# A decoder step on one core: the residual add before the FFN on VectorE alone, its squares summed behind the last block, the third norm's root spread one column block later

## The chip, the cores and the metric

The kernel runs on one core of a Trainium2 chip. The metric is the time of one execution on the device, in microseconds (us); the figure for the kernel before is the median of three executions. A profile of one execution, taken by the hardware profiler, lists every instruction with its start and its length. The engines are named as in the profile: PE is TensorE's matmul, PEld its weight load, DVE is VectorE, ACT is ScalarE, POOL is GpSimd, and SP issues most DMAs.

## What is computed

One inference step of one decoder layer, for 256 prompt tokens and 8 sequences of 8 new tokens: 320 tokens, width 2048, all in float32. Cut to the part around the change:

```python
def decoder_layer(x, ssm_state, ssm_conv_state, ffn_conv_state, p):
    h = rms_norm(x, p["norm_mix_pre"])
    ...                              # two head groups, from h
    mix = jnp.concatenate([gate_out, ssm_out], axis=-1) @ p["w_out"]
    x = x + rms_norm(mix, p["norm_mix_post"])          # called x1 below
    f, new_ffn_conv = conv_ffn(rms_norm(x, p["norm_ffn_pre"]), ffn_conv_state, ...)
    x = x + rms_norm(f, p["norm_ffn_post"])

def conv_ffn(h, conv_state, w_up, conv_w, conv_b, w_down):
    up = h @ w_up                                      # 2048 -> 2 x 5632 columns
    up, new_conv = causal_depthwise_conv(up, conv_state, conv_w, conv_b)
    g, u = jnp.split(up, 2, axis=-1)
    return (jax.nn.gelu(g, approximate=True) * u) @ w_down, new_conv
```

`rms_norm(x, w)` is `x * rsqrt(mean(x*x) + 1e-6) * w`. The norm that the FFN reads (the third of the layer's four) has its token factor, the rsqrt, pulled out: the kernel multiplies x1 by the weight alone, projects that, and multiplies the projected columns by the factor, called `r3`, when it reads them out of PSUM.

## The kernel before, and what sets the order

Everything is held transposed: 128 of the 2048 features lie on the partitions, the 320 tokens along the free axis, so x1 is 16 blocks of 128 x 320 (`acc[:, kt, :]`, kt from 0 to 15).

**Products.** float32 products are made of three passes: each weight tile and each activation block is split into a rounded part `hi` and the remainder `lo`, and `accumulate` (L126 to L130) adds hi·hi (L128), hi·lo (L129) and lo·hi (L130) in PSUM. `slab` (L110) fetches one weight tile of 128 x 1024, i.e. eight blocks of 128 x 128: a DMA issued by SP into `wraw` (L115), a cast on ACT to `whi` (L117), a subtraction on DVE to `wlo` (L119). Each has three buffers, so ACT may cast tile n + 3 only when PE is done with tile n. Eight blocks of three passes are 24 matmuls.

**The first six column blocks.** `project` (L152) is called at L1030 for the FFN's first group. It makes four column blocks of the gate half, and, with `more`, two of the other half, in 12 weight tiles: x1's blocks 0-1, 2-3, then the two extra columns for blocks 0-3, then 4-5, 6-7, the extra columns for 4-7, and 8-9, 10-11, extra for 8-11; the last four blocks, 12-15, come in two tiles for the four columns and one for the extra. The results stay in PSUM (`late=up0`, six banks: four of pool `mm`, two of pool `ms`, which has four as well).

**x1's blocks.** `x1_ready` (L1017) makes them a cut ahead: DVE scales the mix by weight and by the second norm's factor, which lies in PSUM (L1022); an add of x, loaded by SP into `xr` in four parts with two buffers (`load_x`, L1013, issue at L1015), gives x1 (L1023), on DVE for blocks 0 and 1 and on POOL for the other 14; `split` makes `h_hi` on ACT (L343) and `h_lo` on DVE (L344). A part of `xr` is reloaded when the last of its four adds is done.

**Squares.** For the third norm, ACT squares each x1 block and POOL adds the even ones up in `sq3`, DVE the odd ones in `sq3b` (`add_square`, L276 to L282, called at L1034). They are queued behind the add of block 11.

**Seventh and eighth column blocks, root and spread.** `ffn_up(0)` (L1086 to L1108) makes them one by one, two weight tiles each: `ps_one` in a bank of pool `ms`, `ps_other` in one of pool `mm`. Written behind half of the seventh block are two `token_sums` (L258, ones-products over the partitions, L263), one for `sq3` and one for `sq3b`; `rsqrt_by_root` (L237) with DVE's L243 and L244, a square root on ACT, a reciprocal and a Newton step on DVE; behind the seventh block, `spread` (L267) transposes the result on PE (L271) and ACT copies it to `r3` (L273). `evac` (L1054) then reads each column block out of PSUM times `r3` (L1062, L1063) and goes on to the convolution and the gelu. The eighth block's bank comes free with the first `evac`; the next group's `project` needs four banks of `mm`.

**Order.** Each engine works through its own queue in order. A planner fixes the queues ahead of time: of what is ready by its own estimate it takes the work with the highest priority, then the earliest in the code. `first()` is the highest, the weight tiles and x1's blocks share the next, everything else comes in the order of the code. `tc.issue_after(ins)` queues the instructions in its block behind `ins` on the same engine, without a wait.

Of the kernel before, what the change touches and what calls it, by code (L numbers as in the profile page):

```python
# [17 lines left out]
P = 128  # L18
# [3 lines left out]
NT = NP + NS  # L22
D = 2048
KD = D // P
# [10 lines left out]
def hybrid_step(  # L35
# [10 lines left out]
    act, dve, pool, pe, sp = nc.scalar, nc.vector, nc.gpsimd, nc.tensor, nc.sync  # L46
# [6 lines left out]
    tp = ctx.enter_context(tc.tile_pool(name="tp", bufs=2))  # L53
# [11 lines left out]
    with tc.high_priority(offset=300000):  # L65
        dve.memset(ones, 1.0)

        ps = misc("early")
# [31 lines left out]
    def col(i):  # L100
        return prm[:, i:i + 1]


    def first():

        return tc.high_priority(offset=200000)
# [19 lines left out]
    def accumulate(ps, w, xhi, xlo, first, last):  # L126
        whi, wlo = w
        pe.matmul(ps, whi, xhi, start=first, stop=False)  # L128
        pe.matmul(ps, whi, xlo, start=False, stop=False)  # L129
        return pe.matmul(ps, wlo, xhi, start=False, stop=last).ins  # L130
# [4 lines left out]
    hT = [None, None]  # L135
# [60 lines left out]
    acc = None  # L196
# [37 lines left out]

    rsqrt_ins, sums_ins = [], []

    def rsqrt_by_root(rest, ps, scale, rows=P):  # L237

        v = tp.tile([P, 3], F32, tag="rs_v3", name="rs_v")[:rows]
        r = tp.tile([P, 3], F32, tag="rs_r3", name="rs_r", bufs=3)[:rows]  # L240
        t = tp.tile([P, 3], F32, tag="rs_t3", name="rs_t")[:rows]
        s = tp.tile([P, 3], F32, tag="rs_s3", name="rs_s")[:rows]
        dve.tensor_scalar(out=v, in0=rest, scalar1=scale, scalar2=EPS, op0=ALU.mult, op1=ALU.add)  # L243
        dve.scalar_tensor_tensor(out=v, in0=ps, scalar=scale, in1=v, op0=ALU.mult, op1=ALU.add)  # L244
        act.activation(s, v, AF.Sqrt)
        dve.reciprocal(r, s)
        dve.scalar_tensor_tensor(out=t, in0=v, scalar=-0.5, in1=r, op0=ALU.mult, op1=ALU.mult)
        dve.tensor_tensor(out=t, in0=t, in1=r, op=ALU.mult)
        rsqrt_ins.append(dve.scalar_tensor_tensor(out=r, in0=t, scalar=1.5, in1=r, op0=ALU.add, op1=ALU.mult).ins)
        return r  # L250
# [7 lines left out]
    def token_sums(*sqs):  # L258

        ps = misc("tsum")  # L260
        for c, o in enumerate((0, P, NT - P)):
            for i, sq in enumerate(sqs):
                ins = pe.matmul(ps[:, c:c + 1], sq[:, o:o + P], ones[:, 0:1], start=i == 0, stop=i == len(sqs) - 1).ins  # L263
        sums_ins.append(ins)
        return ps[:, 0:3]

    def spread(r, out=None):  # L267

        ps = misc("spread")
        for c, o in ((2, NT - P), (0, 0), (1, P)):  # L270
            pe.transpose(ps[:, o:o + P], r[:, c:c + 1].to_broadcast([P, P]), ident)  # L271
        if out is not None:
            act.copy(out, ps[:, :NT])  # L273
        return ps[:, :NT]

    def add_square(total, x, begins, adder=pool, place=("sq", 2)):  # L276
        if begins:
            act.activation(total, x, AF.Square)
        else:
            sq = tp.tile([P, NT], F32, tag=place[0], name="sq", bufs=place[1])  # L280
            act.activation(sq, x, AF.Square)
            adder.tensor_tensor(out=total, in0=total, in1=sq, op=ALU.add)  # L282

    def squares_of(total):
# [3 lines left out]
        def step(nb):  # L288
# [3 lines left out]
            with first():  # L292
# [5 lines left out]
                if nb > KD - 3:  # L298
# [12 lines left out]
    acc = hp.tile([P, KD, NT], F32, name="acc_mix")  # L311
# [3 lines left out]
    prm_at = dict(zip(("norm", "sc", "fw0", "fw1", "fw2", "fb"),  # L315
                      ((0, KD, 2 * KD, 3 * KD), (4 * KD, 4 * KD + 96), *((4 * KD + 120 + 2 * NF * i,) for i in range(4)))))
# [20 lines left out]
    def split(hi, lo, x, scale=None):  # L337

        if scale is None:
            act.copy(hi, x)  # L340
            dve.tensor_tensor(out=lo, in0=x, in1=hi.bitcast(F32), op=ALU.subtract)
        else:
            act.activation(hi, x, AF.Copy, scale=scale)  # L343
            dve.scalar_tensor_tensor(out=lo, in0=x, scalar=scale, in1=hi.bitcast(F32), op0=ALU.mult, op1=ALU.subtract)  # L344

    def out_parts(pool_, name):
        return (pool_.tile([P, 4, NT], F32R, tag=f"{name}hi", name=f"{name}hi"),
# [14 lines left out]
    with ExitStack() as mctx:  # L362
        op = mctx.enter_context(tc.tile_pool(name="op", bufs=1))
# [138 lines left out]
        with tc.tile_pool(name="gp", bufs=1) as gp:  # L502
# [11 lines left out]
            k = 0  # L514
# [168 lines left out]
            hi, lo = res  # L683


        with tc.tile_pool(name="sd", bufs=1) as sd:
# [8 lines left out]
            for c in range(4):  # L695
                ps = misc("bt_ps")
# [14 lines left out]
            rest = []  # L711
# [256 lines left out]
            norm = heads_out(0, 2, 2)  # L968
# [3 lines left out]
            norm = heads_out(1, 2, 2)  # L972
# [3 lines left out]
            norm = heads_out(2, 2, 3)  # L976
# [16 lines left out]
            with first():  # L993
                with tc.issue_after(pd_last[-1]):
                    made = next(rest[0])
                with tc.issue_after(made):
                    most = token_sums(sq2)
                with tc.issue_after(sums_ins[-1]):
                    ps = token_sums(*one)
                with tc.issue_after(sums_ins[-1]):  # L1000
                    made = next(rest[1])
                r = rsqrt_by_root(most, ps, 1.0 / D)
                behind = rsqrt_ins[-1]
                with tc.issue_after(behind):
                    next(rest[1])
                with tc.issue_after(made):
                    r2b = spread(r)
            sq3 = hp.tile([P, NT], F32, tag="ssq", name="sq3")


            xr, added = {}, []

            def load_x(q):  # L1013
                xr[q] = op.tile([P, 4, NT], F32, tag="xs", name="xr", bufs=2)
# [2 lines left out]
            def x1_ready(k0, nk):  # L1017
                for kt in range(k0, k0 + nk):
                    q, k = kt // 4, kt % 4
                    a = acc[:, kt, :]  # L1020
                    with first() if kt < 2 else tc.high_priority(offset=100000):
                        dve.scalar_tensor_tensor(out=a, in0=a, scalar=col(prm_at["norm"][0] + kt), in1=r2b, op0=ALU.mult, op1=ALU.mult)  # L1022
                        added.append((dve if kt < 2 else pool).tensor_tensor(out=a, in0=a, in1=xr[q][:, k, :], op=ALU.add).ins)  # L1023
                        split(hT[0][:, kt, :], hT[1][:, kt, :], a, col(prm_at["norm"][1] + kt))
                        if k == 3 and q < 2:
                            load_x(q + 2)
            load_x(0)
            load_x(1)
            up0 = []
            project(ffn_w_up, 0, None, late=up0, ready=x1_ready, after=behind, ahead=1, more=DFF, held=added)  # L1030
            sq3b = tp.tile([P, NT], F32, tag="pv", name="sq3b", bufs=4)
            with tc.issue_after(added[11]):
                for kt in range(KD):
                    add_square((sq3, sq3b)[kt % 2], acc[:, kt, :], kt < 2, (pool, dve)[kt % 2], ("pv", 4))  # L1034
    x1 = acc


    with tc.tile_pool(name="fp", bufs=1) as fp:
        r3 = fp.tile([P, NT], F32, name="r3")
# [4 lines left out]
        def ffn_up(g):  # L1044
            fst = fp.tile([P, 2, 4, NB, 2], F32, tag="fst", name="fst", bufs=2)
            for half in range(2):
                k = NF * half + 4 * g
# [3 lines left out]
            hi = fp.tile([P, 4, NT], F32R, tag="fhi", name="fhi", bufs=2)  # L1051
# [34 lines left out]
            if g == 0:  # L1086

                ps = misc("ps_one")
                for i in range(2):
                    wb = slab(rows_of(ffn_w_up, 8 * i, 8, DFF + 256, P))  # L1090
                    for k in range(8):
                        kt = 8 * i + k
                        accumulate(ps[:, :NT], wb(k, 0), hT[0][:, kt, :], hT[1][:, kt, :], kt == 0, kt == KD - 1)
                    if i == 0:
                        with first():
                            r = rsqrt_by_root(token_sums(sq3), token_sums(sq3b), 1.0 / D)
                with first():
                    spread(r, r3)
                up0.append((None, 6, ps))
                for _, j, ps in up0:  # L1100
                    evac(j // 4, j % 4, ps)
                ps = mm.tile([P, 512], F32, tag="mm", name="ps_other")
                for i in range(2):
                    wb = slab(rows_of(ffn_w_up, 8 * i, 8, DFF + 384, P))
                    for k in range(8):
                        kt = 8 * i + k
                        accumulate(ps[:, :NT], wb(k, 0), hT[0][:, kt, :], hT[1][:, kt, :], kt == 0, kt == KD - 1)
                evac(1, 3, ps)  # L1108
            else:
                for half in range(2):  # L1110
                    project(ffn_w_up, DFF * half + 512 * g, lambda j, ps: evac(half, j, ps))

            for half in range(2):
                k = NF * half + 4 * g
# [14 lines left out]
        for g in range(NG):  # L1129
            hi, lo = nxt  # L1130
            if g < NG - 1:
                nxt = ffn_up(g + 1)
            if g == 0:
                acc = fp.tile([P, KD, NT], F32, name="acc_ffn")
# [15 lines left out]
        with tc.issue_after(pd_last[-1]):  # L1150
            most = token_sums(sq4)
        with tc.issue_after(sums_ins[-1]):
            made = hand_over(banks, 0)
        with tc.issue_after(made):
            ps = token_sums(*one)
        r = rsqrt_by_root(most, ps, 1.0 / D)
        with tc.issue_after(sums_ins[-1]):
            made = hand_over(banks, 1, 2)
        with tc.issue_after(made):
# [105 lines left out]
```

## Time and profile before

| | |
|---|---|
| executions, us | 1821.31, 1821.66, 1822.76 |
| median, us | 1821.66 |
| span of the profiled execution, first to last instruction, us | 1821.3 |
| mean granted TensorE clock | 0.993 |
| weight bytes and other reads from HBM, MB | 277.80 |

The profiled execution's span is given and not its full time; the three executions lie 0.0 to 1.5 us above that span. Rows of the profile are read like this: a group has its line, engine, operation, the tiles written and read with their shapes, the count, then busy us and mean ns of one, then the engine's idle time just ahead of them and what ended it. A row of a timeline has start, length, engine, line, operation; a bracket holds the idle time before it and who ended it. "PEclk" is the share of full TensorE clock that the throttle granted.

### The profile page before, as it was taken

Reading aid. Unit: us, or ns where it says so; the run is one execution under the profiler, and the core shown is the slowest. Engines: PE = TensorE matmul, PEld = TensorE weight load, DVE = VectorE, ACT = ScalarE, POOL = GpSimd, SP = SyncE. Lnnn points to the kernel's source line nnn. Section 1 sums busy time; section 2 is a strip of 40 time slices with the busy share of each in tenths; the row PEclk is TensorE's granted clock in tenths of the full one; section 3 lists DMA queues with packets and bytes.
Section 4 is the critical chain, followed back from the end, with each engine's and each line's share of the span. In section 5 each row is a group of like instructions: output and inputs, shape, how many; then the busy total and the mean of one; then the engine's idle time right before and its main releaser. Section 6 shows DMA issues by size and latency. Waiting matters only on the chain.

```text
span 1821.3 us, 31186 instructions
## 1 busy us (share of the span) xinstructions
PE 1789.4 (98%) x12222; PEld 1751.6 (96%) x12222; DVE 1182.3 (65%) x2029; ACT 798.1 (44%) x1102; POOL 304.5 (17%) x626
## 2 busy tenths in 40 slices
PE   8999999999999999999899999999999999999998
PEld 8999999999889899999899999999999999999997
DVE  5449664557977868677776465647465665756575
ACT  6444454334535445444455433333334343433334
POOL 3102200000331312104521010101111010101004
PEclk9999999999999999999999999999999999999999
DMA  8656544455566565556454545444545445454542
GB/s 268 186 150 189 159 132 152 155 157 176 189 192 189 162 196 173 156 159 206 148 149 151 150 153 153 151 152 151 153 152 154 150 154 150 151 148 153 151 154 99
DMA packets 222947, 294.66 MB, mean 162 GB/s; under 512 B 16752, under 2 KB 150736, under 8 KB 222608
## 3 DMA queue, kind: packets, MB, share of 16 engines
q1 hardware_dynamic: 210544, 270.21, 48.6%
q10 hardware_dynamic: 9872, 14.82, 2.2%
q0 software_dynamic: 2384, 7.64, 1.4%
q8 instruction: 96, 1.57, 0.4%
q14 instruction: 51, 0.42, 0.1%
HBM read 277.80 MB, written 14.82 MB: 161 GB/s over the span
## 4 chain that ended last, share of the span: by engine, by line
PE 88%; DVE 4%; DMA 2%; issue 2%; POOL 2%; ACT 1%; ACTq 0%; POOLq 0%; DVEq 0%
PE ps L128 18%; PE ps L130 18%; PE ps L129 18%; PE pd L128 9%; PE pd L130 9%; PE pd L129 9%; DVE wlo L119 1%; PE y_ps L888 1%; DMA cT<-in_x_tok 1%; POOL acc_mix L1023 1%; ACT whi L117 1%; DMA cs<-dacs_d 1%; DMA st<-in_state_ssm 0%; POOL st L808 0%; PE sg L650 0%
## 5 line engine op out<-in xcount | busy, mean ns | idle before, releaser
L119 DVE TENSOR_TENSOR wlo<-wraw,whi 128x1024 fp32r<-128x1024 f32 (+1 forms) x476 | 592.0, 1244 | 455.4 <-ACT whi L117 452.8
L117 ACT CAST whi<-wraw 128x1024 fp32r<-128x1024 f32 (+1 forms) x476 | 496.3, 1043 | 730.2 <-PE ps L129 443.7
L128 PE MATMUL ps<-h_hi,whi 128*128 128x320 f32 x2528 | 787.5, 312 | 8.6 <-ACT whi L117 5.6
L130 PE MATMUL ps<-h_hi,wlo 128*128 128x320 f32 x2528 | 783.9, 310 | 4.3 <-DVE wlo L119 4.3
L129 PE MATMUL ps<-h_lo,whi 128*128 128x320 f32 x2528 | 782.8, 310 | 0.0
L128 PEld LDWEIGHTS ps<-h_hi,whi 128*128 128x128 f32 x2528 | 477.5, 189 | 14.2 <-ACT whi L117 6.9
L130 PEld LDWEIGHTS ps<-h_hi,wlo 128*128 128x128 f32 x2528 | 477.2, 189 | 6.6 <-DVE wlo L119 6.4
L129 PEld LDWEIGHTS ps<-h_lo,whi 128*128 128x128 f32 x2528 | 477.5, 189 | 0.7 <-issue 0.5
L128 PE MATMUL pd<-fhi,whi 128*128 128x320 f32 x704 | 217.0, 308 | 0.0
L129 PE MATMUL pd<-flo,whi 128*128 128x320 f32 x704 | 217.0, 308 | 0.0
L130 PE MATMUL pd<-fhi,wlo 128*128 128x320 f32 x704 | 217.0, 308 | 0.0
L128 PE MATMUL pd<-ohi,whi 128*128 128x320 f32 x448 | 140.8, 314 | 0.0
L129 PE MATMUL pd<-olo,whi 128*128 128x320 f32 x448 | 139.5, 311 | 0.0
L130 PE MATMUL pd<-ohi,wlo 128*128 128x320 f32 x448 | 139.4, 311 | 0.0
L128 PEld LDWEIGHTS pd<-fhi,whi 128*128 128x128 f32 x704 | 132.1, 188 | 0.0
L129 PEld LDWEIGHTS pd<-flo,whi 128*128 128x128 f32 x704 | 132.1, 188 | 0.0
L130 PEld LDWEIGHTS pd<-fhi,wlo 128*128 128x128 f32 x704 | 132.1, 188 | 0.0
L1074 POOL COPY ptf<-pad 128x2 f32<-128x2 f32 x88 | 20.5, 233 | 618.1 <-DVE pad L1062 617.4
L211 DVE TENSOR_TENSOR acc_ffn<-acc_ffn,pd 128x320 f32<-128x320 f32 x160 | 77.5, 484 | 38.7 <-PE pd L130 37.4
L128 PEld LDWEIGHTS pd<-ohi,whi 128*128 128x128 f32 x448 | 84.8, 189 | 2.9 <-issue 1.6
L130 PEld LDWEIGHTS pd<-ohi,wlo 128*128 128x128 f32 x448 | 84.7, 189 | 1.0 <-issue 1.0
L129 PEld LDWEIGHTS pd<-olo,whi 128*128 128x128 f32 x448 | 84.8, 189 | 0.5 <-issue 0.2
(297 smaller groups left out, 1599.4 us busy)
## 6 DMA issues: line engine op xcount, KB each, us to landing
wraw<-in_ffn_w_up SPq DMA_DIRECT2D x176, 512.0 KB, 3.7
wraw<-in_w_in SPq DMA_DIRECT2D x144, 512.0 KB, 3.7
wraw<-in_ffn_w_down SPq DMA_DIRECT2D x88, 512.0 KB, 3.5
wraw<-in_w_out SPq DMA_DIRECT2D x64, 512.0 KB, 3.5
st<-in_state_ssm SPq DMA_DIRECT2D x40, 256.0 KB, 3.8
out_ssm_state_sample<-st ACTq DMA_DIRECT2D x30, 256.0 KB, 3.6
cs<-dacs_d SPq DMA_DIRECT2D x16, 320.0 KB, 4.3
xr<-in_xT SPq DMA_DIRECT2D x4, 640.0 KB, 4.8
```

Source lines behind the costliest of these rows:

```text
L117: act.copy(hi[:, :m], raw[:, :m])
L119: dve.tensor_tensor(out=lo[:, :m], in0=raw[:, :m], in1=hi[:, :m].bitcast(F32), op=ALU.subtract)
L128: pe.matmul(ps, whi, xhi, start=first, stop=False)
L129: pe.matmul(ps, whi, xlo, start=False, stop=False)
L130: return pe.matmul(ps, wlo, xhi, start=False, stop=last).ins
L211: dve.tensor_tensor(out=acc[:, nb, :], in0=acc[:, nb, :], in1=ps[:, :NT], op=ALU.add)
L888: pe.matmul(ps[64 * i:64 * i + 64, cols], w(hl), x(hl, m, cpx), tile_position=(0, 64 * i), **flags)
L1023: added.append((dve if kt < 2 else pool).tensor_tensor(out=a, in0=a, in1=xr[q][:, k, :], op=ALU.add).ins)
L1074: pool.tensor_copy(ptf[:, k, :], pad[:, 256:258])
```

## The change

All of x1's adds go to DVE (L1023). The squares are summed by DVE alone, into one tile `sq3`: the first five are queued behind block 11 (the add on DVE, the cast `h_hi` on ACT), the other eleven behind block 15's cast on ACT. There is one token sum in place of two, so `rsqrt_by_root` drops L244 where no second sum is given. In the code the sum stands behind the seventh block, and the spread, with the reads that need it, behind half of the eighth. ACT copies column block 0 out of PSUM into a new SBUF tile `raw`, from which its `evac` then reads.

```diff
-    def rsqrt_by_root(rest, ps, scale, rows=P):
+    def rsqrt_by_root(rest, scale, ps=None, rows=P):
...
-        dve.scalar_tensor_tensor(out=v, in0=ps, scalar=scale, in1=v, op0=ALU.mult, op1=ALU.add)
+        if ps is not None:
+            dve.scalar_tensor_tensor(out=v, in0=ps, scalar=scale, in1=v, op0=ALU.mult, op1=ALU.add)
...
-            act.activation(hi, x, AF.Copy, scale=scale)
+            made = act.activation(hi, x, AF.Copy, scale=scale).ins
             dve.scalar_tensor_tensor(out=lo, in0=x, scalar=scale, in1=hi.bitcast(F32), op0=ALU.mult, op1=ALU.subtract)
+            return made
...
-                        added.append((dve if kt < 2 else pool).tensor_tensor(out=a, in0=a, in1=xr[q][:, k, :], op=ALU.add).ins)
-                        split(hT[0][:, kt, :], hT[1][:, kt, :], a, col(prm_at["norm"][1] + kt))
+                        added.append(dve.tensor_tensor(out=a, in0=a, in1=xr[q][:, k, :], op=ALU.add).ins)
+                        whole.append(split(hT[0][:, kt, :], hT[1][:, kt, :], a, col(prm_at["norm"][1] + kt)))
...
-            sq3b = tp.tile([P, NT], F32, tag="pv", name="sq3b", bufs=4)
-            with tc.issue_after(added[11]):
-                for kt in range(KD):
-                    add_square((sq3, sq3b)[kt % 2], acc[:, kt, :], kt < 2, (pool, dve)[kt % 2], ("pv", 4))
+            for kt in range(KD):
+                with tc.issue_after(added[11]), tc.issue_after(whole[11 if kt < 5 else KD - 1]):
+                    add_square(sq3, acc[:, kt, :], kt < 1, dve, ("pv", 4))
...
-                    if i == 0:
-                        with first():
-                            r = rsqrt_by_root(token_sums(sq3), token_sums(sq3b), 1.0 / D)
+                up0.append((None, 6, ps))
+                raw = fp.tile([P, NT], F32, name="raw")
+                act.copy(raw, up0[0][2][:, :NT])
+                up0[0] = (None, 0, raw)
                 with first():
-                    spread(r, r3)
-                up0.append((None, 6, ps))
-                for _, j, ps in up0:
-                    evac(j // 4, j % 4, ps)
+                    r = rsqrt_by_root(token_sums(sq3), 1.0 / D)
                 ps = mm.tile([P, 512], F32, tag="mm", name="ps_other")
                 for i in range(2):
...
+                    if i == 0:
+                        with first():
+                            spread(r, r3)
+                        for _, j, up in up0:
+                            evac(j // 4, j % 4, up)
                 evac(1, 3, ps)
```

The two other calls of `rsqrt_by_root` (L1002, L1156) only pass their arguments in the new order.

More of the change, by code (lines that the diff above doesn't have):

```diff
@@ L1001, in hybrid_step @@
                     made = next(rest[1])
-                r = rsqrt_by_root(most, ps, 1.0 / D)
+                r = rsqrt_by_root(most, 1.0 / D, ps)
                 behind = rsqrt_ins[-1]
@@ L1008, in hybrid_step @@
             sq3 = hp.tile([P, NT], F32, tag="ssq", name="sq3")
-            xr, added = {}, []
+            xr, added, whole = {}, [], []
             def load_x(q):
@@ L1155, in hybrid_step @@
             ps = token_sums(*one)
-        r = rsqrt_by_root(most, ps, 1.0 / D)
+        r = rsqrt_by_root(most, 1.0 / D, ps)
         with tc.issue_after(sums_ins[-1]):
```

## The prediction

> **What bounds the kernel now.** I read the page first, then busy times by stretch, then TensorE's timeline where it waits, then who it waits for.
>
> ```profile
> span 1821.3 us, 31186 instructions
> PE 1789.4 (98%) x12222; PEld 1751.6 (96%) x12222; DVE 1182.3 (65%) x2029; ACT 798.1 (44%) x1102; POOL 304.5 (17%) x626
> PE 88%; DVE 4%; DMA 2%; issue 2%; POOL 2%; ACT 1%; ACTq 0%; POOLq 0%; DVEq 0%
> ```
>
> PE is the bound: 98% busy, 88% of the chain that ended last. A change elsewhere is worth what it takes out of PE's waits. POOL, busy 17%, has 2% of that chain, so somewhere PE hangs on it. The stretches around the FFN's first six column blocks (us, then busy time of PE, PEld, DVE, ACT, POOL, then the granted clock) show where:
>
> ```profile
> 862.40:866.00 3.60, 3.60 (x15) 3.60 (x16) 3.57 (x7) 2.20 (x6) 2.44 (x3) 0.56 0.00 0
> 866.00:888.40 22.40, 22.40 (x154) 22.40 (x154) 20.21 (x25) 11.00 (x19) 13.63 (x12) 1.00 0.56 176
> 888.40:903.10 14.70, 9.34 (x57) 8.03 (x56) 10.20 (x13) 8.84 (x17) 9.93 (x17) 1.00 0.28 82
> 903.10:906.60 3.50, 3.50 (x15) 3.50 (x14) 2.69 (x3) 0.69 (x1) 0.07 (x1) 0.51 0.66 189
> ```
>
> PE is fed until 888.4, then idles 14.70 − 9.34 = 5.36 us, and then 3.5 us run at a granted clock of 0.51. In PE's timeline the idle time is five waits, each ended by ACT's or DVE's half of a weight tile:
>
> ```profile
> 888.41 0.31 PE L130 MATMUL ps<-h_hi,wlo 128*128 128x320 f32 x1
> 889.53 0.41 PE L128 MATMUL ps<-h_hi,whi 128*128 128x320 f32 x1 [0.81 <-ACT whi L117]
> 891.51 0.41 PE L130 MATMUL ps<-h_hi,wlo 128*128 128x320 f32 x1 [1.42 <-DVE wlo L119]
> 895.58 0.41 PE L130 MATMUL ps<-h_hi,wlo 128*128 128x320 f32 x1 [0.29 <-DVE wlo L119]
> 901.23 0.41 PE L128 MATMUL ps<-h_hi,whi 128*128 128x320 f32 x1 [2.14 <-ACT whi L117]
> 902.49 0.41 PE L130 MATMUL ps<-h_hi,wlo 128*128 128x320 f32 x1 [0.70 <-DVE wlo L119]
> 906.62 0.31 PE L129 MATMUL ps<-h_lo,whi 128*128 128x320 f32 x1
> 914.24 0.31 PE L130 MATMUL ps<-h_hi,wlo 128*128 128x320 f32 x1
> ```
>
> ACT and DVE are late because their queues stand behind POOL. The waits of 862 to 904 (total us, times, longest), and the groups of 860 to 904 (busy us, mean ns | idle before, and on whom), with one group of the whole run for comparison last:
>
> ```profile
> ACT sq L281 <- POOL sq L282: 3.7, 2, 2.7
> DVE h_lo L344 <- ACT h_hi L343: 1.0, 3, 0.4
> L343 ACT ACTIVATE h_hi<-acc_mix,prm 128x320 fp32r<-128x320 f32 x16 | 8.9, 563 | 17.8 <-POOL acc_mix L1023 15.0 <-DVE acc_mix L1023 2.9
> L1023 POOL TENSOR_TENSOR acc_mix<-acc_mix,xr 128x320 f32<-128x320 f32 x14 | 15.9, 1154 | 10.0 <-DVE acc_mix L1022 10.0
> L282 POOL TENSOR_TENSOR sq<-sq,sq 128x320 f32<-128x320 f32 x7 | 7.9, 1135 | 3.9 <-ACT sq L281 3.9
> L119 DVE TENSOR_TENSOR wlo<-wraw,whi 128x1024 fp32r<-128x1024 f32 x9 | 13.6, 1514 | 2.3 <-ACT whi L117 2.3
> L344 DVE SCALAR_TENSOR_TENSOR h_lo<-acc_mix,prm,h_hi 128x320 fp32r<-128x320 f32 x16 | 12.6, 809 | 1.0 <-ACT h_hi L343 1.0
> L1022 DVE SCALAR_TENSOR_TENSOR acc_mix<-acc_mix,prm,spread 128x320 f32<-128x320 f32 x16 | 8.0, 540 | 0.0
> L344 DVE SCALAR_TENSOR_TENSOR h_lo<-xs,prm,h_hi 128x320 fp32r<-128x320 f32 x4 | 2.1, 546 | 0.0
> ```
>
> POOL costs twice. ACT waits 15.0 us for its adds and 3.7 us for its squares, and a weight cast queued behind such a wait is late: with three buffers, the one that PE lacks at 888.41 had been free for two tiles of work. And DVE, reading two SBUF tensors while POOL does, is stretched: L344 takes 809 ns here, 546 elsewhere; L1022, whose other input is in PSUM, keeps 540.
>
> Here the Trainium skill can be weighed (SBUF — State Buffer, section "SBUF: two separate sides"): DVE and GpSimd contend for a shared port pair held for a whole instruction, by a DVE instruction with two SBUF inputs too. The 809 against 546 ns agree. If the stretch had another cause it would stay, which is the second rival below.
>
> **The change part by part.**
>
> *The loss that can go.* Full-clock matmuls start (914.24 − 906.62)/52 = 0.1466 us apart. A weight tile is 24 of them, 3.52 us; the stage has 12 tiles. At 888.41 seven are done, so 5 × 24 = 120 starts remain, due to end at 888.41 + 17.59 = 906.00; the last is at 914.24. **Lost: 8.24 us.** The parts agree: 5.36 idle, 3.5 × (1 − 0.51) = 1.7 of slow clock behind the waits, and about 0.26 for each of five restarts (a 0.41 us matmul, and an idle counted from an end that overlaps the next start), 1.3; together 8.4. The slow 3.6 us from 862.40 follow PE's wait for x1's first block, which the change leaves: not counted.
>
> *Adds to DVE.* 14 of 16 adds leave POOL. On DVE, intervals come from these rows:
>
> ```profile
> 860.32 1.01 DVE L1022 SCALAR_TENSOR_TENSOR acc_mix<-acc_mix,prm,spread 128x320 f32<-128x320 f32 x2
> 861.24 0.89 DVE L1023 TENSOR_TENSOR acc_mix<-acc_mix,xr 128x320 f32<-128x320 f32 x2
> 862.04 0.54 DVE L1022 SCALAR_TENSOR_TENSOR acc_mix<-acc_mix,prm,spread 128x320 f32<-128x320 f32 x1
> 868.71 1.00 DVE L344 SCALAR_TENSOR_TENSOR h_lo<-acc_mix,prm,h_hi 128x320 fp32r<-128x320 f32 x2
> 869.63 0.99 DVE L1022 SCALAR_TENSOR_TENSOR acc_mix<-acc_mix,prm,spread 128x320 f32<-128x320 f32 x2
> 894.30 1.22 DVE L119 TENSOR_TENSOR wlo<-wraw,whi 128x1024 fp32r<-128x1024 f32 x1
> 895.44 1.09 DVE L282 TENSOR_TENSOR sq3b<-sq3b,sq 128x320 f32<-128x320 f32 x2
> ```
>
> So 0.46 for L1022, 0.40 for the add, 0.46 for L344, 1.14 for an undisturbed weight subtraction. One block costs DVE 1.32 us, all 16 21.1. Queued behind each DVE add are the next subtractions and scalings, and PE waits for the former. The tight point is the eighth tile, due at 888.41: by then DVE may, in the order of the code, have all 16 blocks and the subtractions of tiles 3 to 8 before it: 21.1 + 6 × 1.14 = 27.9, from 860.32 to 888.2. That is even with PE. L344's waits for ACT (1.0 us in all before) can push it past; blocks 12 to 15 are needed only two tiles later, at 888.41 + 2 × 3.52 = 895.4, so where the subtraction slips in between, nothing is late. Bounds: no wait to the 0.81 + 1.42 = 2.23 of today at that tile; I take **0.5 us**, near the 0, since most of the 1.0 us can be filled with other ready work.
>
> After that tile DVE has little to do: 2 × 1.14 per 7 us. The add also frees xr's buffers, whose reloads are issued by SP:
>
> ```profile
> xr<-in_xT SPq DMA_DIRECT2D x4, 640.0 KB, 4.8
> 872.97 0.34 SPq L1015 DMA_DIRECT2D xr<-in_xT  x1
> ```
>
> The last reload was issued at 872.97, behind block 7's add. By DVE's rate block 7 is added near 860.3 + 8 × 1.32 + 2 × 1.14 = 873.2: the same; it lands 4.8 later, at 878, and block 12 comes at about 882. Cost 0. SP's weight loads queue behind it as before.
>
> *Squares.* POOL's 7 adds and DVE's 7 become 15 on DVE: 8 × 0.40 = 3.2 us more, behind x1's blocks and at low priority. The first five come after block 11, the other eleven after block 15, near 888: 11 × 0.40 + 4 tiles × 1.14 = 9.0, so the sum stands at about 897, and the seventh block begins near 906: covered by 9 us. Uncovered, PE would wait one for one.
>
> *Token sums and root.* The second sum (3 products) and DVE's L244 go:
>
> ```profile
> 914.39 0.31 PE L128 MATMUL ps_one<-h_hi,whi 128*128 128x320 f32 x1
> 914.54 0.73 PE L263 MATMUL tsum<-ones,sq 128*128 128x1 f32 x6
> 915.13 0.39 PE L129 MATMUL ps_one<-h_lo,whi 128*128 128x320 f32 x1
> 915.36 0.31 PE L130 MATMUL ps_one<-h_hi,wlo 128*128 128x320 f32 x1
> 919.10 0.43 ACT L273 COPY r<-spread 128x320 f32<-128x320 f32 x1 [2.28 <-PE spread L271]
> 926.66 0.42 DVE L1062 TENSOR_TENSOR pad<-ps,r 128x256 f32<-128x256 f32 x1
> 930.44 0.43 DVE L1062 TENSOR_TENSOR pad<-ps_other,r 128x256 f32<-128x256 f32 x1 [0.20 <-PE ps_other L130]
> ```
>
> A sum pushes the next matmul back by 915.13 − 914.54 = 0.59, and the one after starts 0.23 later instead of 0.147: **0.67 us off PE**. The code had the sum behind half a block, yet it ran behind the first matmul, being of highest priority; I expect that again, at about 906.8. From there to r3 it took 919.53 − 914.54 = 5.0 with two sums; without the second about 4: r3 at 911. The copy of block 0 into `raw` is 0.42 us of ACT (L273 is one such copy), idle there, and frees a PSUM bank before r3 for the eighth block: 0.
>
> *Sum.* −8.24 − 0.67 + 0.5 = **−8.4 us**. All later work is PE at its own rate, so nothing gives it back. The profiled span is 1821.3; the runs are 1821.31 to 1822.76, so little lies around it. Span: 1812.9; from the median 1821.66: **1813.3 us**.
>
> **The rivals.** A measurement here tells about 0.2%, 3.6 us, from no change.
>
> 1. *r3 comes late and banks run out.* If the spread ran where the code has it, behind half of the eighth block, r3 stands at 906.7 + 0.67 + 7.04 + 3.52 + about 1 for the spread and its copy = 918.9. The next group needs a fourth bank, the eighth block's, 18 matmuls after 921.8, at 924.4. r3 to the sixth and seventh blocks' reads took 926.66 − 919.53 = 7.1 us, the eighth's 10.9 (waiting for PE). So the bank is free between 927.6 and 930.8: 3.2 to 6.4 us lost, 4.4 taken nearer the lower: 1817.7. For it: the place in the code. Against: the sum ran early before. Chance 0.08.
> 2. *The waits do not go.* Either DVE's instructions stay at 809 and 1514 ns for a cause other than POOL (16 × 0.26 + 6 × 0.29 = 5.9 us past the eighth tile), or the two waits at 901 to 902 are the weight loads' own (2.14 + 0.70, 1.7 of slow clock, two restarts: 5.1); 5.3 between them: 1818.6. Against: casts that start right after POOL's waits. Chance 0.12.
> 3. *Slower: DVE's queue becomes the bound.* If each block runs unpipelined, L1022, add, ACT's cast, L344 one after the other, it costs 0.54 + 0.49 (0.89 for two, less 0.40) + 0.56 + 0.55 and some 0.3 of hand-overs, an estimate, 2.4 us; 16 × 2.4 + 12 × 1.14 + 15 × 0.40 = 58 us against the 52 from 862.4 to 914.4: 6 us slower, 1827.7. It decides from (52 − 13.7 − 6)/16 = 2.0 us per block. Against: two blocks' steps already interleave in the rows at 860.32 to 862.04. The Trainium skill (Perfetto Trace Analysis, section "Tensor Engine Instruction") calls DVE and ACT strict FIFO, the rule that speaks for this rival; the late casts here agree. Chance 0.10.
>
> **How the numbers follow.** Forecast 0.70, with 1812.0 to 1815.5 of its own (no wait at the eighth tile is 1812.8, all 2.23 is 1815.0, and the runs spread by about half a us either way). With the first rival, range 1812.0 to 1818.0, 0.78 and the nearer half of the second. Faster is the forecast and the first rival, 0.78; same is the second, 0.12; slower the third, 0.10.
>
> **What would show it.** Right: no L1023 or L282 on POOL, L344 near 550 and L119 near 1230 ns in the stage; PE's starts 0.147 apart from 866 to about 906; one sum right behind the first matmul of the seventh block, r3 near 911, no wait at the next group. Wrong: PE idle between 888 and 906 behind DVE's L119 (rival 3, or a wrong 0.5), a granted clock near 0.5 there, a sum or spread that PE waits for, or PE idle around 924.

## The result, and the profile after

| | before | after | |
|---|---|---|---|
| median, us | 1822.21 (1821.31 to 1823.06, 4 runs) | 1812.57 (1810.76 to 1813.45, 4 runs) | ratio 0.9947, 95% [0.9935, 0.996] |
| profiled execution: span / time, us | 1821.3 / 1823.06 | 1809.0 / 1810.76 | |

The change makes the kernel 9.6 us faster (7.3 to 11.8); 8.4 were forecast. Measured twice more, beside the experiments below, it gave ratios of 0.9959 [0.9947, 0.9972] and 0.9955 [0.9942, 0.9967], which are 7.5 and 8.2 us of 1821.66. Lines behind the edits have moved by one or two: `h_lo` is L345, the scaling L1024, the add L1025, the square's sum L283, the token sum L264, the spread L272.

The page after, its span and busy times:

```profile
span 1809.0 us, 31182 instructions
PE 1781.5 (98%) x12216; PEld 1744.9 (96%) x12216; DVE 1182.6 (65%) x2050; ACT 798.0 (44%) x1103; POOL 284.5 (16%) x605
```

PE still fills 98% of the span, which is 12.3 us shorter; POOL has 20 us less to do. The same stretches of the first six column blocks as before the change (us, busy of PE, PEld, DVE, ACT, POOL, then the granted clock):

```profile
859.00:862.90 3.90, 3.85 (x16) 3.85 (x17) 3.90 (x10) 1.46 (x3) 0.00 (x0) 0.56 0.17 23
862.90:886.30 23.40, 23.40 (x161) 23.40 (x161) 21.27 (x39) 14.45 (x24) 0.23 (x5) 1.00 0.52 168
886.30:887.00 0.70, 0.70 (x7) 0.70 (x6) 0.70 (x3) 0.18 (x1) 0.61 (x1) 1.00 0.32 69
887.00:902.90 15.90, 15.90 (x110) 15.90 (x109) 14.30 (x22) 8.52 (x16) 4.99 (x5) 1.00 0.68 201
```

PE is fed from 859.05 to the end; the five waits are gone and so is the half clock behind them. Only the half clock at the start is left. DVE's groups of 857 to 901 (total, mean ns | idle before, on whom):

```profile
L119 DVE TENSOR_TENSOR wlo<-wraw,whi 128x1024 fp32r<-128x1024 f32 x11 | 13.3, 1218 | 0.1
L1024 DVE SCALAR_TENSOR_TENSOR acc_mix<-acc_mix,prm,spread 128x320 f32<-128x320 f32 x16 | 8.1, 542 | 0.0
L345 DVE SCALAR_TENSOR_TENSOR h_lo<-acc_mix,prm,h_hi 128x320 fp32r<-128x320 f32 x16 | 8.0, 546 | 2.1 <-ACT h_hi L344 2.1
L283 DVE TENSOR_TENSOR sq<-sq,sq 128x320 f32<-128x320 f32 x15 | 7.4, 490 | 1.0
L1025 DVE TENSOR_TENSOR acc_mix<-acc_mix,xr 128x320 f32<-128x320 f32 x16 | 7.0, 485 | 0.0
```

The weight subtraction and `h_lo` have their undisturbed lengths, 1218 and 546 ns, where they had 1514 and 809. PE's timeline at the eighth tile's first three remainders, at the end of the sixth block, and at the next group:

```profile
885.92 0.31 PE L130 MATMUL ps<-h_hi,wlo 128*128 128x320 f32 x1
...
886.21 0.31 PE L129 MATMUL ps<-h_lo,whi 128*128 128x320 f32 x1
886.36 0.46 PE L130 MATMUL ps<-h_hi,wlo 128*128 128x320 f32 x2
886.65 0.31 PE L128 MATMUL ps<-h_hi,whi 128*128 128x320 f32 x1
...
902.93 0.31 PE L128 MATMUL ps_one<-h_hi,whi 128*128 128x320 f32 x1
903.08 0.72 PE L264 MATMUL tsum<-ones,sq 128*128 128x1 f32 x6
903.66 0.39 PE L129 MATMUL ps_one<-h_lo,whi 128*128 128x320 f32 x1
...
906.53 0.49 PE L272 MATMUL spread<-ident,rs_r 128*128 128x128 f32 x3
...
917.86 0.31 PE L130 MATMUL ps_other<-h_hi,wlo 128*128 128x320 f32 x1
918.00 0.31 PE L128 MATMUL ps<-h_hi,whi 128*128 128x320 f32 x1
```

Two starts take 886.65 − 886.36 = 0.29, and no line has a bracket: no wait at the eighth tile. The stage took 902.93 − 859.05 = 43.88 us, and from there to the next group 918.00 − 902.93 = 15.07. Before, the same points give 862.37 (start), 52.02 and 15.80. So of the 12.3 us between the two profiled spans 8.14 are the stage and 0.73 the second part. Of the rest, 3.3 lie ahead of the stage, where both kernels have the same instructions in the same order; the runs below show that its start moves by itself.

### The profile page after: what moved, and what is told of

Its sections match the earlier page's. It is cut to its first block, busy times and chain, and to the rows that moved or that the text cites. A ratio compares the mean times of both kernels' runs of the same rounds, so it can differ in the third digit from the quotient of the medians.

```text
span 1809.0 us, 31182 instructions
## 1 busy us (share of the span) xinstructions
PE 1781.5 (98%) x12216; PEld 1744.9 (96%) x12216; DVE 1182.6 (65%) x2050; ACT 798.0 (44%) x1103; POOL 284.5 (16%) x605
## 4 chain that ended last, share of the span: by engine, by line
PE 88%; DVE 4%; DMA 4%; issue 2%; ACT 1%; POOL 1%; ACTq 0%; SPq 0%; POOLq 0%; DVEq 0%
PE ps L128 19%; PE ps L129 19%; PE ps L130 19%; PE pd L128 9%; PE pd L130 9%; PE pd L129 9%; DVE wlo L119 1%; DMA cs<-dacs_d 1%; PE y_ps L890 1%; DMA st<-in_state_ssm 1%; DMA cT<-in_x_tok 1%; ACT whi L117 1%; POOL st L810 0%; PE sg L652 0%; DMA out_ssm_state_sample<-st 0%
```

## The experiments

**How they are read.** For each kernel the stage (first matmul of the six blocks to first of the seventh) and the second part (to the next group's first matmul) come from PE's timeline. The half clock at the start is the time from the first matmul until windows of 0.4 us show PEclk 1.00. At PE's rate the stage is 12 × 24 × 0.1466 = 42.2 us; a half clock of h us makes that h/2 longer, so the next-to-last column, stage − h/2, is what to compare with 42.2. It is good to about 0.3. "11 behind block 15" means that eleven of the sixteen squares are queued there and five behind block 11.

| kernel | adds | squares' sums | stage | half clock h | stage − h/2 | second |
|---|---|---|---|---|---|---|
| before | POOL | POOL and DVE, behind block 11 | 52.02 | 3.3 | **50.4** | 15.80 |
| e1 | DVE | as before | 44.16 | 4.1 | **42.1** | 15.79 |
| e2 | POOL | DVE, 11 behind block 15 | 44.96 | 5.2 | **42.4** | 15.08 |
| e5 | POOL | DVE, behind block 11 | 45.00 | 5.7 | **42.2** | 15.08 |
| e6 | POOL | POOL and DVE, 11 behind block 15 | 48.19 | 4.9 | **45.7** | 15.79 |
| e8 | POOL | POOL and DVE, all behind block 15 | 49.30 | 3.6 | **47.5** | 15.80 |
| e10 | POOL | as e8, more buffers | 48.73 | 3.3 | **47.1** | 15.80 |
| e3 | DVE, POOL made busy | DVE | 47.95 | 6.1 | **44.9** | 15.09 |
| e4 | DVE | DVE; root and spread at the old place | 43.88 | 3.7 | **42.0** | 15.09 |
| after | DVE | DVE | 43.88 | 3.9 | **41.9** | 15.07 |

Besides the half clock at the start, the clock fell a second time inside the stage in three kernels: in before, e8 and e10, for 3.4 us each, from 903.2, 898.6 and 897.6. That is 1.7 us of their bold numbers; without it before has 48.7, e8 45.8 and e10 45.4, beside e6's 45.7.

*Theory at the outset:* POOL's two kinds of work, x1's adds and the squares' sums, each delay ACT and stretch DVE, and the loss goes as they leave. *Rival:* one of them alone carries it, or something else (the place of the squares, the root and spread).

**e1, adds only.** Before, with one line changed:

```diff
-  added.append((dve if kt < 2 else pool).tensor_tensor(...
+  added.append(dve.tensor_tensor(...
```

> The kernel before with one part of the change alone: all adds of x on DVE; squares on POOL and DVE and both token sums as before. Measured in the profile: the stage from the first matmul of the six column blocks to the first of the seventh (52.02 us before, 43.88 after the change), and from there to the next group (15.80 before, 15.07 after). Theory (POOL's adds hold up ACT's casts, and nothing else in the stage binds): PE waits behind the eighth tile go; POOL's seven square adds still stand between ACT's squares and its casts and still stretch DVE, but late, where there is slack: stage 44 to 45.5, second part 15.8, time 1814 to 1815.5. Rival (the squares make the late waits by themselves): 2.14 + 0.70 of wait, 1.7 of slow clock and two restarts stay, stage 49, time about 1818.

Measured: 1812.02 us (1810.95 to 1813.44), ratio 0.9942 [0.9927, 0.9957]; stage 44.16, second part 15.79. The stage loss is gone with the adds alone, and the second token sum alone stays: 0.7 us. The squares still made ACT wait 3.4 us for POOL, and no one on PE noticed.

**e2, adds back on POOL.** The changed kernel, with that one line undone.

> The changed kernel with 14 of 16 adds back on POOL; squares on DVE alone behind the last block, one token sum and the late spread stay. Theory: the adds' part of the loss comes back, since ACT waits for POOL again: PE waits at the eighth tile by 1 to 2.5 us and DVE's h_lo takes 800 ns, but nothing waits for POOL's squares any more; stage 46 to 49, second part 15.1, time 1815 to 1818. Rival (the squares were the whole loss): stage 44, time 1812.6. If it comes out near 52, the adds alone make all of the loss and the squares none.

Measured: 1811.78 us (1810.96 to 1814.09), 0.9942 [0.9927, 0.9957]; stage 44.96. **A miss of the theory.** DVE's `h_lo` is stretched as before (801 ns beside 809), its weight subtraction less (1392 ns, between 1218 and 1514), and ACT waits for POOL's adds 12.1 us where it waited 15.0. From DVE's groups of the stage:

```profile
L119 DVE TENSOR_TENSOR wlo<-wraw,whi 128x1024 fp32r<-128x1024 f32 x11 | 15.2, 1392 | 0.4 <-ACT whi L117 0.4
L345 DVE SCALAR_TENSOR_TENSOR h_lo<-acc_mix,prm,h_hi 128x320 fp32r<-128x320 f32 x16 | 12.4, 801 | 1.0 <-ACT h_hi L344 1.0
```

and from its waits (total us, times, longest):

```profile
ACT h_hi L344 <- POOL acc_mix L1025: 12.1, 12, 1.7
```

Yet PE never waits after its start, and what the stage has over the changed kernel's 43.88 is its longer half clock. So either part of the change alone brings all of the stage's gain. The loss was an interaction.

**e3, POOL made busy.** The changed kernel, and behind each of 14 adds on DVE an addition on POOL of the same size, whose result nobody reads:

```diff
+  if kt > 1:
+      pool.tensor_tensor(out=r1, in0=a, in1=a, op=ALU.add)
```

> The changed kernel with 14 more adds of 128x320 on POOL (x1's block plus itself, into a tile that nothing reads), so POOL is as busy in the stage as before and no engine waits for it. They add work that the result does not need. It tells the two ways apart in which POOL can cost: held-up queues or stretched DVE instructions. If the stretch matters: DVE's two-input instructions (add, h_lo, weight subtraction) grow from 485, 546 and 1218 ns to about 800, 800 and 1500, DVE passes the eighth tile some 5 us late, stage 47 to 49, time 1816 to 1818. If only the queues matter: stage 43.9 to 44.5, time 1812.6 to 1813.2, whatever the lengths.

Measured: 1815.47 us (1814.07 to 1815.92), 0.9962 [0.9947, 0.9976]; stage 47.95. PE's timeline where it waits:

```profile
888.38 0.42 PE L130 MATMUL ps<-h_hi,wlo 128*128 128x320 f32 x1 [0.69 <-DVE wlo L119]
893.24 0.41 PE L130 MATMUL ps<-h_hi,wlo 128*128 128x320 f32 x1 [1.35 <-DVE wlo L119]
```

and the group of DVE's `h_lo`:

```profile
L345 DVE SCALAR_TENSOR_TENSOR h_lo<-acc_mix,prm,h_hi 128x320 fp32r<-128x320 f32 x16 | 12.4, 817 | 1.2 <-ACT h_hi L344 1.2
```

No engine waits for POOL in this stage, so POOL costs here through the stretch alone: 44.9 − 42.2 = 2.7 us, the place being the eighth and the ninth tile's subtraction, the latter behind four `h_lo` that take 3.78 us. The Trainium skill (SBUF — State Buffer, section "SBUF: two separate sides") has a DVE instruction with two SBUF inputs and a GpSimd one that reads SBUF lock one port pair, each for its whole length. The trace agrees: 546 ns become 801 (e2) and 817 (e3) when POOL works beside, wherever its work comes from.

**e4, root and spread back.** The changed kernel with the token sum, the spread and the reads of PSUM at their old places in the code, and without `raw`.

> The changed kernel with the root and the spread back at their places in the code (the sum behind half of the seventh block, the spread behind the seventh, no copy into raw); the adds and the squares stay on DVE, one token sum. Theory: the sum and the spread run as early as their inputs allow in both, so the later place in the code and the copy are worth nothing: stage 43.9, second part 15.1, time 1812.6 within 0.6. Rival (the move keeps PE from a wait for the sum, or frees the bank of the eighth block): PE waits 1 to 4 us at the seventh or eighth block, second part 16 to 19, time 1814 to 1817.

Measured: 1812.02 us (1811.07 to 1813.92), 0.9943 [0.9928, 0.9957]; stage 43.88, second part 15.09. This part of the change is worth nothing: the planner had put the sum behind the first matmul of the seventh block and the spread inside that block already before the change, and it does after it.

**e5, e6, e8: is it the place, or the adder?** With the adds on POOL, e5 sums the squares on DVE but early; e6 splits them as before but late; e8 puts all of them last:

```diff
# e5, against e2
-  with tc.issue_after(added[11]), tc.issue_after(whole[11 if kt < 5 else KD - 1]):
+  with tc.issue_after(added[11]):
# e6, against e2 (and the second token sum); e8 has whole[KD - 1] for all
-      add_square(sq3, acc[:, kt, :], kt < 1, dve, ("pv", 4))
+      add_square((sq3, sq3b)[kt % 2], acc[:, kt, :], kt < 2, (pool, dve)[kt % 2], ("pv", 4))
```

> The changed kernel with the 14 adds back on POOL and all squares summed by DVE, but all of them queued behind block 11's add as in the kernel before, not eleven of them behind block 15's cast. Only the adder differs from before in the squares. If what cost time before was POOL holding both the adds and the squares in one queue (theory): the stage stays near 45 to 46.5 us, time within 2 us of the changed kernel. Rival, the place of the squares ahead of the last blocks' casts on ACT and ahead of their h_lo on DVE costs by itself: stage 48 us or more, time 1815 or more.

> The changed kernel with the 14 adds back on POOL and the squares split between POOL and DVE as before, with the two token sums, but eleven of the squares queued behind block 15's cast on ACT. Only the place differs from before in the squares. Theory (adds and squares must stand together in POOL's queue to cost time): POOL makes its seven square adds after its last x1 add, so no cast of a block waits for a square and the stage is 45 to 46 us; the second sum gives 0.7 us back (15.8 us from the seventh block to the next group). Rival, POOL's squares beside DVE are enough wherever they stand: stage 48 to 52 us.

> As the run with the squares split and eleven of them late, but all sixteen queued behind block 15's cast on ACT, so that no square stands ahead of any x1 add on POOL. That run had one, at 882.42 us, ahead of block 15's add, and squares beside the last blocks' subtractions; its stage took 48.19 us, 45.7 without the half clock at its start. Theory (adds and squares mixed in POOL's queue, and POOL's squares beside the blocks' work on DVE, cost time together): stage without its start's half clock 42.2 to 43 us (288 starts at 0.1466 are 42.2), second part 15.8 us. Rival, POOL's squares stretch the weight subtractions wherever they stand: 44 us or more without the half clock, and the sum may come late for the seventh column block.

Measured: e5 1812.63 us (1810.9 to 1815.22), 0.9958 [0.9945, 0.9972]; e6 1817.15 (1814.57 to 1819.63), 0.9978 [0.9969, 0.9987]; e8 1817.92 (1815.92 to 1820.64), 0.9984 [0.9975, 0.9993]. The place of the squares is worth nothing when DVE sums them (e5 against e2). Split with POOL they cost, wherever they stand; that the two must be mixed in POOL's queue, the theory by then, **fell with e8** (e6 still had one of POOL's sums ahead of block 15's add). How much they cost does depend on the place: without the half clocks, 48.7 in before, 45.7 in e6 and 45.8 in e8. In e8, ACT's timeline:

```profile
889.09 1.04 ACT L117 CAST whi<-wraw 128x1024 fp32r<-128x1024 f32 x1
890.03 0.47 ACT L282 ACTIVATE sq<-acc_mix 128x320 f32<-128x320 f32 x1
892.76 0.83 ACT L282 ACTIVATE sq<-acc_mix 128x320 f32<-128x320 f32 x2 [2.26 <-POOL sq L283]
894.23 0.83 ACT L282 ACTIVATE sq<-acc_mix 128x320 f32<-128x320 f32 x2 [0.64 <-POOL sq L283]
895.66 0.47 ACT L282 ACTIVATE sq<-acc_mix 128x320 f32<-128x320 f32 x1 [0.61 <-POOL sq L283]
896.04 1.03 ACT L117 CAST whi<-wraw 128x1024 fp32r<-128x1024 f32 x1
```

and PE's, for that cast:

```profile
897.12 0.41 PE L128 MATMUL ps<-h_hi,whi 128*128 128x320 f32 x1 [2.15 <-ACT whi L117]
898.38 0.43 PE L130 MATMUL ps<-h_hi,wlo 128*128 128x320 f32 x1 [0.70 <-DVE wlo L119]
```

The same 2.1 and 0.7 stood in the profile of before, at 901 to 902. The tenth tile's cast stands in ACT's queue behind squares that wait for a buffer, which POOL's sum frees.

That sum itself stood behind other work of POOL's. POOL's timeline of e8:

```profile
889.47 2.41 POOL L1062 COPY pad<-fst 128x16 f32<-128x16 f32 x4
891.85 0.88 POOL L283 TENSOR_TENSOR sq<-sq,sq 128x320 f32<-128x320 f32 x1
```

and of before:

```profile
894.50 2.22 POOL L1060 COPY pad<-fst 128x16 f32<-128x16 f32 x5 [2.03 <-DMA fst<-in_fconv]
896.68 0.88 POOL L282 TENSOR_TENSOR sq<-sq,sq 128x320 f32<-128x320 f32 x1
```

In both, the sum for which ACT waits longest (2.26 and 2.70 us) stands behind copies of the convolution's state, which are neither adds nor squares; in before these had waited for a DMA. No run moves the copies by themselves, so what part of the loss is theirs stays open.

Why the two halves don't add up shows in how far ahead of PE that cast starts. The tenth tile's first matmul is the 217th of the stage:

| kernel | cast starts | PE would use it | ahead, us |
|---|---|---|---|
| after: neither on POOL | 885.43 | 892.4 | 6.9 |
| e1: squares split, adds on DVE | 887.44 | 894.4 | 6.9 |
| e2, e5: adds on POOL, squares on DVE | 890.22, 890.96 | 892.7, 893.7 | 2.5, 2.8 |
| e8, before: both | 896.04, 900.14 | used at 897.12, 901.23 | late |

The cast itself takes 1.04 us, so of a lead of 6.9 some 5.9 are to spare. The adds on POOL use up 4.1 to 4.4 of it; PE doesn't see it. The squares' waits, 3.4 us in e1 and 4.4 in e8, are also under 5.9 by themselves; in e1 they come behind this tile's cast, and the twelfth tile's, behind 2.5 us of them, still starts 4.7 ahead of its use. In e8 three of them, 3.5 us, come ahead of the tenth tile's cast: with the adds' 4.4 that is, as an estimate from these figures, 7.9 against 5.9, 2.0 too much, and PE waits 2.15 there.

**e10, more buffers.** e8 with eight of ACT's squares in buffers of their own, so that the cast needn't stand behind a wait:

```diff
+  own = [op.tile([P, 4, NT], F32, tag="xs", name="sqx", bufs=2) for _ in range(2)]
...
+      if 2 <= kt < 10:
+          to = own[(kt - 2) // 4][:, (kt - 2) % 4, :]
+          act.activation(to, acc[:, kt, :], AF.Square)
+          (pool, dve)[kt % 2].tensor_tensor(out=(sq3, sq3b)[kt % 2], in0=(sq3, sq3b)[kt % 2], in1=to, op=ALU.add)
```

> The run with all squares split between POOL and DVE behind the last cast, and eight of its sixteen squares written by ACT into buffers of their own (those of x's last two parts, free by then) in place of the four that they shared. There ACT waited 4.4 us for POOL's sums, the tenth weight tile's cast began only at 896.04 us, behind two such waits, and PE waited 2.15 and 0.70 us for it. Theory, what costs time is the weight cast that stands behind those waits in ACT's queue: with the buffers ACT does not wait ahead of that cast, PE's wait of 2.15 us and the half clock behind it go, and the stage without its start's half clock is 42.2 to 43 us. Rival, DVE's subtractions, stretched beside POOL, are late by themselves: PE still waits 1.5 us or more for wlo, and the stage without the half clock is 44.5 us or more. The second token sum stays: 15.8 us behind the stage, or more if POOL's sum is late.

Measured: 1817.99 us (1815.84 to 1820.45), 0.998 [0.997, 0.9989]; stage 48.73. **The theory's cast came in time and the time did not change** (e8 had 1817.92). ACT's timeline has the tenth tile's cast at 891.80, 2.9 us ahead of PE's first use of it at 894.73:

```profile
891.80 1.04 ACT L117 CAST whi<-wraw 128x1024 fp32r<-128x1024 f32 x1
```

DVE's has what stands ahead of that tile's subtraction:

```profile
891.27 3.33 DVE L1040 TENSOR_TENSOR sq3b<-sq3b,sqx 128x320 f32<-128x320 f32 x3
894.70 0.49 DVE L283 TENSOR_TENSOR sq3b<-sq3b,sq 128x320 f32<-128x320 f32 x1
895.11 1.89 DVE L119 TENSOR_TENSOR wlo<-wraw,whi 128x1024 fp32r<-128x1024 f32 x1
```

and PE waits for it:

```profile
897.05 0.41 PE L130 MATMUL ps<-h_hi,wlo 128*128 128x320 f32 x1 [1.87 <-DVE wlo L119]
```

With ACT free, DVE is late: its three sums take 1.11 us each beside POOL's, where the same sum takes 0.49 alone, and the tenth subtraction 1.89. So ACT's wait is not the cause by itself: with it gone, DVE's late subtraction takes its place. Nor does it take POOL's copies: here they stand behind the sums that ACT waits for, at 897.67. DVE's stretch alone, without ACT's waits for POOL, cost 2.7 us in e3. What share each has in the loss of before stays open; a run with ACT's waits and without the stretch is lacking.

**e7, e9: the half clock at the start.** One more loss was left in the changed kernel. e7 puts ten transposes that nobody reads behind the second norm's spread, in PE's wait for x1's first block; e9 puts three more ahead of that spread and eleven behind:

```diff
+    made = warm(ones[:, 0:1], made, 3)       # e9 alone
...
     r2b = spread(r)
+    warm(r[:, 0:1], spread_ins[-1], 11)       # e7: 10
...
+def warm(r, behind, n):
+    ps = misc("warm")
+    with tc.issue_after(behind):
+        for _ in range(n):
+            made = pe.transpose(ps[:, :P], r.to_broadcast([P, P]), ident)
+    return made.ins
```

> The changed kernel and ten transposes more on PE, right behind the spread, in the 2.1 us in which PE waits for x1's first block; nothing reads them. In the changed kernel the first 3.9 us of the six column blocks run at a granted clock of 0.50 to 0.56, which costs about 1.7 us. Theory: the clock fell since PE idled three times in the 5 us before, and work there keeps it up: the stage is 42.3 to 43 us and the time 1 to 1.6 us under the changed kernel's. Rival, the clock follows something else, or had fallen already ahead of the gap: stage 43.9 and no difference, or up to 0.3 us slower where the transposes run on into the stage.

> The changed kernel once more, beside the one with the gap filled and with another profile. The stage should again take 43.9 us and the part up to the next group 15.1 us; what lies before the stage should vary: its start lay at 862.37 us in the one profile of the kernel before and at 859.05 in the one of the changed kernel, with the same instructions up to there on each engine.

> The run with the gap filled, and three transposes more on PE in the 0.52 us ahead of the spread, eleven behind it. There the clock fell to 0.50 at about 858.2 us, inside the fill, and was full again at 861.6, 0.9 us into the stage. Theory A, the fall answers to PE's two waits of 0.34 and 0.52 us ahead of the spread: without the second the clock stays at 1.00, and the stage takes 42.2 to 42.5 us. Theory B, the fall answers to something earlier or comes at a time of its own (the sums' short matmuls, the column blocks before): it falls all the same, for about 3.4 us if PE is fed, and the stage takes 42.5 to 43.5 us as its place happens to lie.

> The changed kernel beside the two. The stage took 43.88 and 43.76 us in its two profiles so far, and the half clock at its start 3.9 and 3.2 us; 43.5 to 45 us expected, and 41.9 to 42.3 without half the half clock's time.

Measured: e7 1810.98 us (1808.99 to 1812.02), stage 42.71, beside the changed kernel's 1813.41 (1810.93 to 1814.16), 43.76. e9 **1808.13** (1807.28 to 1811.27), 0.9934 [0.992, 0.9947], stage 42.34, beside 1812.33 (1810.71 to 1814.49), 0.9955 [0.9942, 0.9967], 43.67. The changed kernel's third profile (same columns as the stretches above):

```profile
857.60:860.80 3.20, 0.65 (x4) 0.30 (x3) 3.07 (x9) 0.55 (x2) 0.54 (x1) 0.94 0.49 182
860.80:863.80 3.00, 2.94 (x11) 2.94 (x12) 3.00 (x8) 1.37 (x4) 0.00 (x0) 0.50 0.01 4
```

and e9's:

```profile
857.90:861.10 3.20, 2.02 (x18) 1.57 (x16) 3.03 (x9) 0.63 (x2) 0.54 (x1) 1.00 0.45 169
861.10:865.00 3.90, 3.90 (x26) 3.90 (x27) 3.90 (x10) 1.40 (x3) 0.00 (x0) 1.00 0.18 21
```

In e7 the clock fell all the same, at 858.2, in the spread just ahead of the fill (858.44 to 860.78); it was back at 861.6, so most of it lay in transposes that nobody waits for. In e9 it stayed at 1.00. By the profile the fill is worth 1.3 us of stage; the medians differ by 4.2, more than the trace explains, and part of that is the spread between executions. That the clock held is one profile, of e9's longest execution (1811.27, mean granted clock 0.996). Its other four have a mean clock of 0.998, the changed kernel's five beside them 0.994 to 0.997; the mean does not say where it held.

The starts of the changed kernel's three profiles, 859.05, 861.85 and 860.87, lie 2.8 us apart with nothing changed. That is near the 3.3 us ahead of the stage in the first comparison.

## Why the prediction was right, and where it was not

*The loss that can go* was right: −8.24 forecast, −8.14 measured. What carries it was right in part: PE's five waits and the half clock behind them are gone, and POOL is what stood behind them. What was put to one side, the half clock at the start, did stay (3.9 us against 3.3).

*"POOL costs twice"* is the step that failed. It took ACT's 15.0 us of waits for the adds and 3.7 for the squares as two costs that go separately. e2 has 12.1 us of such waits, and 801 ns for `h_lo`, and PE is fed throughout: waits of a feeder are no loss while it is ahead. The forecast came out since the change takes both away, each of which would have been enough; that the error did not show in the number is luck. Whoever prices one part of the change by that step is wrong, as the expectation of e2 was.

*Adds to DVE*: the price held. From the first scaling at 857.00 to the last `h_lo` at 887.4, the 16 blocks and six subtractions kept DVE busy for 28.3 us (27.9 forecast), and it waited 2.1 for ACT. The eighth tile's wait, taken at **+0.5 us**, was mis-sized: it was 0, since the subtraction slipped in ahead of the last four `h_lo`, a case that the prediction names:

```profile
884.31 1.22 DVE L119 TENSOR_TENSOR wlo<-wraw,whi 128x1024 fp32r<-128x1024 f32 x1
```

It ends at 885.53, 0.39 ahead of PE's first use. The reload of `xr` cost nothing, as said.

*Squares.* The sum was to stand at 897, with 9 us of cover. DVE's last four sums:

```profile
899.02 2.27 DVE L283 TENSOR_TENSOR sq<-sq,sq 128x320 f32<-128x320 f32 x4
```

They end at 901.29 and the token sum begins at 903.08: 1.8 us of cover, not 9. ACT makes the squares, and its queue had stood for 3.13 us behind a weight cast that waited for its DMA:

```profile
889.61 1.06 ACT L117 CAST whi<-wraw 128x1024 fp32r<-128x1024 f32 x1 [3.13 <-DMA wraw<-in_ffn_w_up]
```

The estimate counted DVE's work alone, and counted four of the sums as done before block 15; all fifteen ran behind it, from 889.56. The cover was there, with little to spare.

*Token sum* −0.67: −0.73 in the trace, 0.71 between e1 and e2. *Root and spread:* 0, shown by e4. r3's copy ends at 907.5; counted from the stage's start that is 910.8 on the time scale of before, forecast 911.

*Sum.* −8.4 was to be set against 1821.66. The text said that little lies around the span; it is 1.76 us (1810.76 − 1809.0), the same in before. The estimate was made as a difference, so it did no harm. Without the mis-sized 0.5 the sum is −8.9, and the two traces give −8.14 − 0.73 = −8.87; the medians' 9.6, 7.5 and 8.2 lie around it.

*Rivals.* The first did not happen: the spread ran inside the seventh block, at 906.53, and the next group waits for no bank. Its price does not follow from its own terms: 918.9 + 7.1 and 918.9 + 10.9 are 926.0 and 929.8, so 1.6 to 5.4 us lost and not 3.2 to 6.4. The second fell: the waits at 901 to 902 were POOL's, its sum behind its copies (e8 has the same two, e5 has none). The third fell: PE waits nowhere for DVE. Its 0.3 us of hand-overs per block came from no row; the one that can be read, from the first add's end (857.92 + 0.49) to ACT's `h_hi` at 858.44, is 0.03. e3 shows what it would have taken, the adds on DVE **and** POOL busy beside it: 2.7 us.

## What to carry to other kernels

A feeder's wait costs only what exceeds its lead over the engine that it feeds: read how far ahead of its use the late cast starts, take off the cast's own length, and price causes together against that lead, not one by one from the table of waits. Where two causes each fit into the lead, removing either brings all of the gain, and the second removal brings nothing (e1 and e2). When one queue's wait is lifted, look for the next one behind it (ACT's cast, then DVE's subtraction) before the gain is counted.

## What the runs showed of the hardware

- The granted clock fell to 0.50 around the start of the stage in every profile but e9's. Where the gap was not filled it came back 3.0 to 6.1 us after PE's first matmul. Counted from its fall it lasted 3.4 us (before, the changed kernel's three profiles, e4, e7, e10) or 6.8 (e1, e2, e3, e5, e6, e8), so what a stage loses is set by how much of that comes after PE's first matmul. In before, e8 and e10 the second fall comes 41.0, 41.0 and 37.6 us after the first, which is 12, 12 and 11 times 3.41. The Trainium skill (TensorE: Matmul & The Clock Gate, section "Part 1: The HAM clock gate (the "warmup" mystery)") names a free-running window of about 3.4 us, idle for the fall and busy for the return. The lengths and the distances agree with the window. e7's half clock from 858.2 to 861.6, with PE fed throughout, agrees with the return. The fall came earlier than that rule: in the changed kernel PE's longest wait there is 2.10 us, behind two of 0.34 and 0.52 within 5 us, and in e7, where that wait was filled, the clock fell behind the 0.34 and the 0.52 alone.
- A sum of 128 x 320 on POOL took 0.86 to 1.11 us (e8); on DVE it takes 0.49 alone, and 1.11 beside POOL's (3.33 for three, e10).
